# Down projection of a ConvGLU: 36 of 44 row blocks as products of seven, in one pipeline with gate and up

## The chip, the core and the metric

The kernel runs on one core of one Trainium2 chip, as one launch. The metric is the time of one execution on the device in microseconds. The profile is of one execution of the kernel before, taken by the hardware profiler. Engines are named as the profile names them: PE (TensorE; PEld are its weight loads), DVE (VectorE), ACT (ScalarE), POOL (GpSimd) and SP (SyncE). SP and POOL issue the DMAs: SP's run on the hardware queue q1, POOL's on the software queue q0.

## What is computed

One trunk layer over 512 positions of width 2048, and a last norm. The change touches the second half of it, the ConvGLU from its weights on, and the last norm:

```python
D_MODEL, SEQ = 2048, 512
D_FF = 5632                       # 44 blocks of 128

def rmsnorm(x, gain):
    return x * lax.rsqrt(jnp.mean(x * x, axis=-1, keepdims=True) + EPS) * gain

def conv_ffn(h, w_gate, w_up, conv_w, conv_b, w_down):
    a = h @ w_gate
    a_pad = jnp.pad(a, ((0, 0), (CONV_WIDTH - 1, 0), (0, 0)))
    a = sum(conv_w[j] * a_pad[:, j:j + L] for j in range(CONV_WIDTH)) + conv_b
    return (jax.nn.silu(a) * (h @ w_up)) @ w_down

# reference(): p = rmsnorm(x) @ w_in; o = concat(hgrn2(p), fox(p))
x = x + o @ w_out
h = rmsnorm(x, norm2_gain)
x = x + conv_ffn(h, w_gate, w_up, conv_w, conv_b, w_down)
return rmsnorm(x, final_norm_gain)
```

## The kernel before

All is float32. A product keeps float32's precision by splitting both operands into a high and a low part of the engine's own format (`split`: hi by ACT, lo = x - hi by DVE) and adding three matmuls: weight hi by input hi, weight hi by input lo, weight lo by input hi (`mms`, L201 to L203). Everything lies transposed, 128 features by 512 positions.

The program runs in this order. The input projection and the two mixers come first. Then `w_out`: sixteen blocks d of 128 outputs, each 16 x 3 matmuls of 512 columns; `x1_out` adds x, writes the sum to DRAM (`x1d`), squares it for the norm, and after every second d makes the "forms" of a pair of blocks.

**Gate and up** are computed as products of seven: the 2 x 2 problem of (up, gate) rows against (first, second) half of the positions, in each pair of input blocks, takes seven products in place of eight, each on a sum of weights (`s1` to `s4`, `a11`, `a12`, `a22`) and a sum of inputs (the forms `b11`, `n2`, `b21`, `t3`, `n1`, `n4`, `b22`; half the positions, 256 columns). The forms, hi and lo, stay in SBUF for the whole stage. For each of the 44 blocks f, `glu(f)` runs seven products of 8 pairs x 3 matmuls of 256 columns (L819 to L821). The four weight matrices of a block are loaded by SP, 512 KB each; `s1` and `s3` are summed by an accumulating DMA that POOL issues (L765), `s2` and `s4` by DVE (L783). `prepare(g + LEAD)` makes the weights' hi (ACT, L807) and lo (DVE, L808) two products ahead. Each f ends with the convolution, SiLU and the product with up, on DVE and ACT; both halves are multiplied by 1/rms of norm 2 there (`R2` for gate, L851, `nR2` for up, L856), split, and written to DRAM (`actd`).

**Down** reads them back. 44 blocks f in NG = 4 groups of GF = 11: for each group and each of 16 blocks d, `unit` runs 11 x 3 matmuls of 512 columns (L201 to L203, `mxt<-ot`); the weights stream in on SP as `raw<-wdn` (512 KB), and DVE adds the sum to `x1[d]`. POOL loads the activations (L886, 256 KB each) and x1 (L893). In the last group twelve d's run so; the last four d are computed with positions on the partitions (L983 to L985), one quarter of the positions at a time, while `norm` (L955 and on) normalizes and writes the quarter before.

On each engine instructions run in the order that the framework's scheduler has given them, in one queue per engine; a wait at the head of a queue holds all that stands behind it. A tile with one buffer can be loaded again only after its last reader.

Of the kernel before, what the change touches and what calls it, by code (L numbers as in the profile page):

```python
# [8 lines left out]
F32 = mybir.dt.float32  # L9
# [6 lines left out]
P = 128  # L16
# [6 lines left out]
GF = 11  # L23
NG = NF // GF
# [12 lines left out]
NPIECE_D = NF * KT * P // PIECE  # L37
QH = T // 2
KP = KT // 2
FORM = KP * P  # L40
LEAD = 2
DMA_SUMS = True
# [11 lines left out]
def tile_hymba_block(ctx: ExitStack, tc: tile.TileContext, xT, wst, wgu, wdn, wfb, consts, out, out_t):  # L54
# [71 lines left out]
    class Stream:  # L126
# [7 lines left out]
        def make(self):  # L134
# [8 lines left out]
            if self.pool is None:  # L143
                hi = self.wp.tile([P, PIECE], F32R, name="whi", tag="whi")
                lo = self.wp.tile([P, PIECE], F32R, name="wlo", tag="wlo")
            else:
                hi, lo = self.pool(F32R), self.pool(F32R)
# [518 lines left out]
    x1d = dr.tile([KT, P, T], F32, name="x1d")  # L666
    actd = dr.tile([NF, 2, P, T], F32, name="actd")
# [14 lines left out]

    tt = opened("tt", 1, "right")
    xr = opened("xr", 1, "right")
    NAMES = ("b11", "n2", "b21", "t3", "n1", "n4", "b22")
    forms = {n: [] for n in NAMES}
    acc2 = tt.tile([P, T], F32, name="acc2")

    def form(name, j, src):
        pool = tt if j < KP - 1 else tl  # L690
        hi = pool.tile([P, QH], F32R, name=f"{name}h{j}")
        lo = pool.tile([P, QH], F32R, name=f"{name}l{j}")
        s.activation(hi, src, AF.Copy)
        v.tensor_tensor(lo, src, f32(hi), op=ALU.subtract)
        forms[name].append((hi, lo))

    def pair_forms(j, ha, hb):
        b11, b12, b21, b22 = ha[:, 0:QH], ha[:, QH:T], hb[:, 0:QH], hb[:, QH:T]
# [4 lines left out]
        form("b11", j, b11)  # L703
# [3 lines left out]
        form("n1", j, n1)  # L707
        form("n2", j, n2)
        form("b21", j, b21)
        v.tensor_tensor(n2, n2, b21, op=ALU.add)  # L710
        form("n4", j, n2)
        t3 = temp()
        v.tensor_tensor(t3, b22, b12, op=ALU.subtract)
        form("t3", j, t3)
        form("b22", j, b22)
# [3 lines left out]
    def x1_out(d, ps):  # L719
# [3 lines left out]
        nc.sync.dma_start(out=x1d[d], in_=t)  # L723
# [10 lines left out]
    for d in range(WOPEN, KT):  # L734
        ps = MM()
        unit(ps, range(KT), os_)
        x1_out(d, ps)
    closed("wp", "wr", "pa")
    tl = opened("tl", 1)
    pair_forms(KP - 1, hg[-2], hg[-1])  # L740
    closed("xr")
    R2 = cp.tile([P, T], F32, name="R2", tag="R")
    nR2 = tl.tile([P, T], F32, name="nR2")

    def put2(u, r0, bc):
        s.activation(R2, bc, AF.Copy)
        s.activation(nR2, bc, AF.Copy, scale=-1.0)
# [3 lines left out]

    wf = opened("wf", 8)
    wh = opened("wh", LEAD + 2)
    gt = opened("gt", 1)
    ORDER = ("a11", "s2", "a12", "s3", "s1", "a22", "s4")
    raw = {}

    def W():
        return wf.tile([P, FORM], F32, name="wq", tag="wq")

    def load(f, name, q, q2=None):
        t = raw[f, name] = W()
        nc.sync.dma_start(out=t, in_=wgu[f, q])
        if q2 is not None:
            gp.dma_start(out=t, in_=wgu[f, q2], accum_op=ALU.add)  # L765

    def loads(f):

        if DMA_SUMS:
            load(f, "s1", 0, 1)  # L770
            load(f, "a11", 2)
            load(f, "s3", 0, 2)
            load(f, "a12", 3)
            load(f, "a22", 1)
        else:
            load(f, "a21", 0)
            load(f, "a22", 1)
            load(f, "a11", 2)
            load(f, "a12", 3)

    def add(f, name, x, y, into=None):
        t = raw[f, name] = W() if into is None else into
        v.tensor_tensor(t, raw[f, x], raw[f, y], op=ALU.add)  # L783

    def sums(f):
        if not DMA_SUMS:
            add(f, "s1", "a21", "a22")
            add(f, "s3", "a21", "a11", raw[f, "a21"])
        add(f, "s2", "s1", "a11")

    ready = {}

    def prepare(g):
        f, i = divmod(g, 7)
        if f >= NF:
            return
        if i == 0:
            sums(f)
            if f + 1 < NF:
                loads(f + 1)  # L800
        name = ORDER[i]
        if name == "s2":
            add(f, "s4", "s2", "a12")
        t = raw.pop((f, name))
        hi = wh.tile([P, FORM], F32R, name="fhi", tag="fhi")
        lo = wh.tile([P, FORM], F32R, name="flo", tag="flo")
        s.activation(hi, t, AF.Copy)  # L807
        v.tensor_tensor(lo, t, f32(hi), op=ALU.subtract)  # L808
        ready[g] = (hi, lo)

    def product(g, ps, first=True):
        prepare(g + LEAD)
        hi, lo = ready.pop(g)
        rhs = forms[NAMES[g % 7]]
        for j in range(KP):
            a, b = hi[:, j * P:(j + 1) * P], lo[:, j * P:(j + 1) * P]
            th, tl = rhs[j]
            kw = {"skip_group_check": not first}
            pe.matmul(ps, lhsT=a, rhs=th, start=(first and j == 0), stop=False, **kw)  # L819
            pe.matmul(ps, lhsT=a, rhs=tl, start=False, stop=False, **kw)  # L820
            pe.matmul(ps, lhsT=b, rhs=th, start=False, stop=(j == KP - 1), **kw)  # L821
            step()
# [4 lines left out]
    def G(name, shape=(P, T), dt=F32):  # L827
        return gt.tile(list(shape), dt, name=name, tag=name)

    def glu(f):  # L830
        cw = con[:, C_CW + 3 * f:C_CW + 3 * f + 3]
        g = 7 * f
        L, H = slice(0, QH), slice(QH, T)
        x, y, z, w = half(mm), half(mx), half(mm), half(mx)
        p1, u2, u3 = (G(n, (P, QH)) for n in ("p1", "u2", "u3"))
        a, uu = G("a"), G("uu")
        product(g, x)
        s.activation(p1, x, AF.Copy)
        product(g + 1, y)
        v.tensor_tensor(u2, p1, y, op=ALU.add)  # L840
        product(g + 2, x, first=False)
        s.activation(a[:, L], x, AF.Copy)
        product(g + 3, y, first=False)
        v.tensor_tensor(u3, p1, y, op=ALU.add)
        product(g + 4, z)
        v.tensor_tensor(uu[:, H], u3, z, op=ALU.add)
        product(g + 5, w)
        v.tensor_tensor(uu[:, L], u3, w, op=ALU.subtract)
        product(g + 6, z, first=False)
# [15 lines left out]
    loads(0)  # L865
    for g in range(LEAD):
        prepare(g)
    for f in range(NF):
        glu(f)
    closed("gt", "wh", "wf", "tl", "tt")  # L870


    wr = opened("wr", 3)
    wp = opened("wp", 4)
    pq = opened("pq", 81, "right")
    ws = Stream(wdn, NPIECE_D, wr, wp)

# [3 lines left out]
    A = X = O  # L881

    def acts_of(f):
        parts = (O(F32R), O(F32R))
        for i, part in enumerate(parts):
            gp.dma_start(out=f32(part), in_=actd[f, i])  # L886
        return parts

    acts = [acts_of(f) for f in range(GF)]
    x1 = []  # L890
    for d in range(KT):
        t = X()
        gp.dma_start(out=t, in_=x1d[d])  # L893
        x1.append(t)
    for g in range(NG - 1):
        nxt = []
        for d in range(KT):
            ps = MX()
            unit(ps, range(GF), acts)
            v.tensor_tensor(x1[d], x1[d], ps, op=ALU.add)  # L900
            if d < GF:
                nxt.append(acts_of((g + 1) * GF + d))
        acts = nxt


    x1t, g3 = [], O()

# [155 lines left out]
```

## Time and profile before

| | us |
|---|---|
| median of 3 runs | 2301.7 (2300.91 to 2302.92) |
| the profiled execution | 2302.55 |
| its span, first to last instruction | 2300.8 |
| last matmul of w_out starts / first product of gate and up starts | 897.5 / 904.7 |
| last matmul of gate and up / first of down | 1785.0 / 1787.9 |
| last matmul of down starts | 2290.5 |

The span is 1.75 us shorter than the time of the same execution; the sum of a prediction is made against 2302.55. A row of a timeline gives the start, the duration, the engine, the line and operation, the tile written and the tiles read, and in brackets the idle time before it and what ended it. Matmuls overlap, so their cost is the distance between two starts, not the duration. [...]

### The profile page before, as it was taken

The page shows a single profiled execution, that of the slowest core. Times are in us where ns is not written, and L with a number is a line of the kernel's source. Part 1 is how long each engine was busy: PE and PEld are TensorE (multiplying, and loading weights), DVE is VectorE, ACT ScalarE, POOL GpSimd, SP SyncE. Part 2 cuts the span into 40 slices and gives each one's busy share as a digit, 9 for nine tenths or more (in the row PEclk, how much of TensorE's full clock was granted, in tenths as well). Part 3 has the DMA queues.
Part 4 walks back from the last instruction along what each step waited for, and adds up shares of the span by engine and source line. Part 5 has one row for each costly group of instructions (what it writes and reads, how often), then busy time and mean ns, then how long its engine had stood idle before and what let it go on. Part 6 is the DMA issues. An engine that isn't in the chain of part 4 may idle for free.

```text
span 2300.8 us, 34411 instructions
## 1 busy us (share of the span) xinstructions
PE 2273.4 (99%) x13662; PEld 2012.7 (87%) x13662; DVE 1464.9 (64%) x2194; ACT 939.2 (41%) x1484; POOL 171.6 (7%) x259
## 2 busy tenths in 40 slices
PE   8999999999999998999999999999999999999998
PEld 7888888788888887999999999999999788888886
DVE  6666467556457565888888888888887333333345
ACT  5333233334335454544444554454444222222234
POOL 4000000000000000000000000000000512000000
PEclk9999999999999999999999999999999999999999
DMA  5222322222222455877877887878784955223223
GB/s 177 83 83 83 100 74 96 74 83 80 86 83 74 142 163 177 226 212 207 216 215 214 212 212 209 216 200 222 208 217 136 375 198 196 92 97 99 85 100 110
DMA packets 112210, 352.67 MB, mean 153 GB/s; under 512 B 12816, under 2 KB 19088, under 8 KB 112048
## 3 DMA queue, kind: packets, MB, share of 16 engines
q1 hardware_dynamic: 89568, 272.67, 36.0%
q0 software_dynamic: 22336, 77.67, 15.4%
q8 instruction: 107, 1.75, 0.3%
q14 instruction: 55, 0.45, 0.1%
q10 hardware_dynamic: 144, 0.12, 0.0%
HBM read 318.96 MB, written 31.46 MB: 152 GB/s over the span
## 4 chain that ended last, share of the span: by engine, by line
PE 95%; DMA 2%; DVE 1%; issue 1%; ACT 0%; POOL 0%; DVEq 0%; ACTq 0%; POOLq 0%
PE pq L819 12%; PE pq L820 12%; PE pq L821 12%; PE mmt L201 9%; PE mmt L203 9%; PE mmt L202 9%; PE mxt L202 7%; PE mxt L201 7%; PE mxt L203 7%; PE mmt L286 2%; PE mmt L284 2%; PE mmt L285 2%; DMA ot<-actd 1%; DMA wq<-wgu 1%; DMA raw<-wdn 1%
## 5 line engine op out<-in xcount | busy, mean ns | idle before, releaser
L150 DVE TENSOR_TENSOR wlo<-raw,whi 128x512 fp32r<-128x512 f32 x453 | 316.3, 699 | 464.5 <-ACT whi L149 424.9
L149 ACT ACTIVATE whi<-raw 128x512 fp32r<-128x512 f32 x453 | 284.8, 630 | 686.3 <-PE mxt L202 322.2
L807 ACT ACTIVATE fhi<-wq 128x1024 fp32r<-128x1024 f32 x308 | 326.6, 1061 | 365.7 <-PE pq L820 323.0
L808 DVE TENSOR_TENSOR flo<-wq,fhi 128x1024 fp32r<-128x1024 f32 x308 | 376.3, 1222 | 58.2 <-ACT fhi L807 52.4
L201 PE MATMUL mmt<-at,whi 128*128 128x512 f32 x896 | 354.8, 396 | 0.0
L203 PE MATMUL mmt<-at,wlo 128*128 128x512 f32 x896 | 349.8, 390 | 0.0
L202 PE MATMUL mmt<-at,whi 128*128 128x512 f32 x896 | 349.3, 390 | 0.0
L201 PE MATMUL mxt<-ot,whi 128*128 128x512 f32 x660 | 262.2, 399 | 2.9 <-ACT whi L149 2.7
L202 PE MATMUL mxt<-ot,whi 128*128 128x512 f32 x660 | 261.8, 397 | 0.5 <-DMA ot<-actd 0.5
L203 PE MATMUL mxt<-ot,wlo 128*128 128x512 f32 x660 | 261.6, 397 | 0.5 <-DVE wlo L150 0.5
L203 PEld LDWEIGHTS mmt<-at,wlo 128*128 128x128 f32 x896 | 168.2, 188 | 35.9
L201 PEld LDWEIGHTS mmt<-at,whi 128*128 128x128 f32 x896 | 168.3, 188 | 34.9 <-issue 1.9
L202 PEld LDWEIGHTS mmt<-at,whi 128*128 128x128 f32 x896 | 168.4, 188 | 33.1
L201 PEld LDWEIGHTS mxt<-ot,whi 128*128 128x128 f32 x660 | 124.5, 189 | 34.8 <-ACT whi L149 2.9
L202 PEld LDWEIGHTS mxt<-ot,whi 128*128 128x128 f32 x660 | 124.6, 189 | 31.8 <-DMA ot<-actd 2.1
L203 PEld LDWEIGHTS mxt<-ot,wlo 128*128 128x128 f32 x660 | 124.7, 189 | 30.6 <-DVE wlo L150 1.0
L765 POOL DMA_DIRECT2D wq<-wgu x88 | 75.9, 862 | 782.1 <-DVE flo L808 388.1
L783 DVE TENSOR_TENSOR wq<-wq 128x1024 f32<-128x1024 f32 x88 | 107.5, 1222 | 3.5 <-DMA wq<-wgu 2.0
L286 PE MATMUL mmt<-wlo,at 128*128 128x512 f32 x256 | 100.6, 394 | 4.4 <-DVE wlo L150 4.4
L819 PE MATMUL pq<-b11h,fhi 128*128 128x256 f32 x352 | 100.2, 285 | 3.6 <-ACT fhi L807 3.6
L284 PE MATMUL mmt<-whi,at 128*128 128x512 f32 x256 | 101.7, 397 | 0.3 <-ACT whi L149 0.3
L821 PE MATMUL pq<-b11h,flo 128*128 128x256 f32 x352 | 99.9, 284 | 1.3 <-DVE flo L808 1.3
(303 smaller groups left out, 5067.7 us busy)
## 6 DMA issues: line engine op xcount, KB each, us to landing
wq<-wgu SPq DMA_DIRECT2D x220, 512.0 KB, 4.5
raw<-wst SPq DMA_DIRECT2D x143, 512.0 KB, 3.5
wq<-wgu POOLq DMA_DIRECT2D x88, 512.0 KB, 7.3
raw<-wdn SPq DMA_DIRECT2D x87, 512.0 KB, 3.5
ot<-actd POOLq DMA_DIRECT2D x88, 256.0 KB, 6.6
actd<-ah SPq DMA_DIRECT2D x44, 256.0 KB, 3.2
actd<-al SPq DMA_DIRECT2D x44, 256.0 KB, 3.0
xt<-xT SPq DMA_DIRECT2D x16, 256.0 KB, 5.3
```

What stands on the lines that cost most here:

```text
L149: s.activation(hi, src, AF.Copy)
L150: v.tensor_tensor(lo, src, f32(hi), op=ALU.subtract)
L201: pe.matmul(ps, lhsT=a, rhs=xh[:, ts], start=(first and i == 0), stop=False)
L202: pe.matmul(ps, lhsT=a, rhs=xl[:, ts], start=False, stop=False)
L203: pe.matmul(ps, lhsT=b, rhs=xh[:, ts], start=False, stop=(last and i == n - 1))
L284: pe.matmul(pss[i], lhsT=xh[:, ts], rhs=hi, start=(k == 0), stop=False)
L286: pe.matmul(pss[i], lhsT=xh[:, ts], rhs=lo, start=False, stop=(k == KT - 1))
L807: s.activation(hi, t, AF.Copy)
L808: v.tensor_tensor(lo, t, f32(hi), op=ALU.subtract)
L819: pe.matmul(ps, lhsT=a, rhs=th, start=(first and j == 0), stop=False, **kw)
L820: pe.matmul(ps, lhsT=a, rhs=tl, start=False, stop=False, **kw)
L821: pe.matmul(ps, lhsT=b, rhs=th, start=False, stop=(j == KP - 1), **kw)
```

## The change

Gate, up and most of down form one pipeline of "units" (`class Seven`): 44 units of gate and up of 7 x 8 x 3 matmuls, then 24 units of down of 7 x 6 x 3 matmuls, all of 256 columns. Down's first 36 row blocks are 18 pairs, in three chunks of six pairs; a unit is one pair of output blocks (m, in the order 6, 7, 0 to 5) of one chunk. Its weight sums are all made on DVE. Its inputs are seven forms of the activations: `forms_out` makes them after each second f and writes them to DRAM (`formd`), and they come back through POOL's queue (`load_form`) into the buffers in which gate and up's forms stood. There is one buffer for each form, so a form of the next chunk is loaded once the product of the chunk's last unit that reads it is through: seven forms, hi and lo, 786 KB each, 11.0 MB per chunk. What a unit gives is added to `yd` in DRAM by an accumulating DMA; in chunk 0 `xi` (x1, multiplied by the rms of norm 2, with its sign turned in the even blocks) is written to `yd` first. The multiplication of up by 1/rms is gone; the last norm applies it. The other 8 row blocks run as before (8 x 3 matmuls of 512 columns for each of twelve d, then the late four). Loads of gate and up's weights are issued in two halves, into 2 + 5 buffers in place of 8.

```diff
-GF = 11
-NG = NF // GF
+FL = 8
+NPIECE_D = FL * KT * P // PIECE
+CHUNKS = (6, 6, 6)
+DORDER = (6, 7, 0, 1, 2, 3, 4, 5)
...
+    class Seven:
+        def loads(self, u, early):
+            src, n, dma_sums = self.units[u]
+            if dma_sums:
+                todo = (("a11", 2), ("s1", 0, 1)) if early else (("a12", 3), ("s3", 0, 2), ("a22", 1))
+            else:
+                todo = (("a11", 2), ("a21", 0)) if early else (("a12", 3), ("a22", 1))
+            for name, q, *more in todo:
+                t = self.tile(u, name)
+                nc.sync.dma_start(out=t, in_=src[q])
+                for q2 in more:
+                    gp.dma_start(out=t, in_=src[q2], accum_op=ALU.add)
...
+        def prepare(self, g):
+            u, i = divmod(g, 7)
+            if i == 0 and not dma_sums:
+                self.sum(u, "s1", "a21", "a22")
+                self.sum(u, "s3", "a21", "a11", into="a21")
+            s.activation(hi, t, AF.Copy)
+            v.tensor_tensor(lo, t, f32(hi), op=ALU.subtract)
+            if i == 0:
+                self.sum(u, "s2", "s1", "a11", into="a11")
+                self.loads(u + 1, True)
+            elif i == 1:
+                self.sum(u, "s4", "s2", "a12", into="s2")
+            elif i == (4 if dma_sums else 3):
+                self.loads(u + 1, False)
...
+    def parts_out(src, n, dst):
+        for i in range(2):
+            t = G("oh" if i == 0 else "ol", (P, 4, QH), F32R)[:, 0:n]
+            if i == 0:
+                hi = t
+                s.activation(t, src, AF.Copy)
+            else:
+                v.tensor_tensor(t, src, f32(hi), op=ALU.subtract)
+            nc.sync.dma_start(out=dst(i), in_=f32(t))
+    def forms_out(p, r):
+        v.tensor_tensor(r[:, 4], r[:, 0], r[:, 1], op=ALU.subtract)
+        v.tensor_tensor(r[:, 1], r[:, 3], r[:, 1], op=ALU.subtract)
+        yield KP
+        v.scalar_tensor_tensor(r[:, 5], r[:, 4], -1.0, r[:, 3], op0=ALU.mult, op1=ALU.subtract)
+        v.tensor_tensor(r[:, 6], r[:, 5], r[:, 2], op=ALU.add)
+        for a, b in ((0, 4), (4, 7)):
+            parts_out(r[:, a:b], b - a, lambda i: formd[c][a:b, i, :, j].rearrange("s p t -> p s t"))
+            yield 2 * KP
+    def load_form(c, name):
+        t = slot(name)
+        for i, part in enumerate(t):
+            gp.dma_start(out=f32(part[:, 0:n]), in_=formd[c][SLOTS.index(name), i])
...
-        v.tensor_tensor(uu, uu, nR2, op=ALU.mult)
-        hi, lo = G("ah", dt=F32R), G("al", dt=F32R)
-        s.activation(hi, uu, AF.Copy)
-        v.tensor_tensor(lo, uu, f32(hi), op=ALU.subtract)
-        for i, part in enumerate((hi, lo)):
-            nc.sync.dma_start(out=actd[f, i], in_=f32(part))
+        if f >= 2 * NPAIR:
+            parts_out(r[:, b:b + 2], 2, lambda i: actd[f - 2 * NPAIR, i])
+        elif f % 2:
+            start(forms_out(f // 2, r))
...
+    def down(c, m, forms, nxt):
+        if c == 0:
+            xi = G("xi", (P, 2, T))
+            gp.dma_start(out=xi, in_=x1d[m])
+            v.scalar_tensor_tensor(xi[:, 0], xi[:, 0], -1.0, rms, op0=ALU.mult, op1=ALU.mult)
+            v.tensor_tensor(xi[:, 1], xi[:, 1], rms, op=ALU.mult)
+            nc.sync.dma_start(out=yd[m], in_=xi)
+        sv.product(x, forms)
+        next_form(nxt, c + 1, 0)
...
+        gp.dma_start(out=yd[m], in_=o, accum_op=ALU.add)
...
-    acts = [acts_of(f) for f in range(GF)]
-    for d in range(KT):
-        gp.dma_start(out=t, in_=x1d[d])
-    for g in range(NG - 1):
-        for d in range(KT):
-            unit(ps, range(GF), acts)
-            v.tensor_tensor(x1[d], x1[d], ps, op=ALU.add)
+    for f in range(FL):
+        for i, part in enumerate(acts[-1]):
+            gp.dma_start(out=f32(part), in_=actd[f, i])
+    for d in (12, 0, 4, 8):
+        for b in range(2):
+            gp.dma_start(out=y4[:, 2 * b:2 * b + 2], in_=yd[d // 2 + b])
...
-    start(norm(i, ps, ys, 6 if i < 3 else 0))
+    start(norm(i, ps, FL + 3 if i < 3 else 0))
```

SP's queue, from the end of w_out to the first weights of gate and up, before. `wq` are weight tiles, `x1d` is the sum after w_out:

```order
L142 DMA raw<-wst 128x1024 [waits DMAHW4_49,DVE_49]
L723 DMA x1d<-xr 128x512 [waits DMAHW0_49,DVE_49]
L763 DMA wq<-wgu 128x1024 [waits PE_49]
L723 DMA x1d<-xr 128x512 [waits DVE_49]
L763 DMA wq<-wgu 128x1024 [waits DMAHW3_49]
```

And after, where `wc` is the tile of `a11`:

```order
L143 DMA raw<-wst 128x1024 [waits DMAHW4_49,DVE_49]
L740 DMA x1d_5869<-xr 128x512 [waits DMAHW0_49,DVE_49]
L790 DMA wc<-wgu 128x1024 [waits PE_49]
L790 DMA wq<-wgu 128x1024
L790 DMA wq<-wgu 128x1024 [waits DMAHW3_49]
L790 DMA wq<-wgu 128x1024
```

The first load of all is now that of `a11`, the second that of `s1`; the wait of the first is for the last matmul of w_out, where before it was for one some 2 us earlier. The last write of x1 stands behind seven loads.

POOL's queue at the end of gate and up, before: all 88 accumulating loads, then the activations of the first group, x1, and the rest.

```order
L765 DMA wq<-wgu 128x1024 x88
L886 DMA ot<-actd 128x512 x22
L893 DMA ot<-x1d 128x512 x16
L886 DMA ot<-actd 128x512 x66
```

And after, from the same place into the second unit of chunk 0 (`formd_5879` is chunk 0's, h and l are hi and lo):

```order
L792 DMA wq<-wgu 128x1024 x88
L905 DMA b11l<-formd_5879 128x1536
L905 DMA b11h<-formd_5879 128x1536
L905 DMA n2h<-formd_5879 128x1536
...
L905 DMA b22h<-formd_5879 128x1536
L905 DMA b22l<-formd_5879 128x1536
L975 DMA xi<-x1d_5868 128x1024
L1003 DMA yd_5876<-o 128x1024
L975 DMA xi<-x1d_5869 128x1024
L975 DMA xi<-x1d_5862 128x1024
```

The fourteen loads of forms (those of `b21`, `t3`, `n1` and `n4` are left out) are followed by the first `xi`; the second `xi` stands behind the accumulation of the first unit's result. At the two later chunk seams the fourteen loads stand behind the accumulation of the last unit but one:

```order
L1003 DMA yd_5874<-o 128x1024
L905 DMA b11l<-formd_5880 128x1536
L905 DMA b11h<-formd_5880 128x1536
...
L905 DMA b22l<-formd_5880 128x1536
L1003 DMA yd_5875<-o 128x1024
```

DVE's queue in chunk 0, in the fourth unit (`flo` are lo parts of weights, L800 sums of weights, `u` and `o` sums of products):

```order
L818 TENSOR_TENSOR flo<-wc,fhi 128x768 [waits Activation_49]
L800 TENSOR_TENSOR wc<-wq,wc 128x768 [waits DVE_49]
L996 TENSOR_TENSOR o<-u_18561,pq 128x256 [waits DMASW1_49,PE_49]
L976 SCALAR_TENSOR_TENSOR xi<-xi,rms 128x512 [waits DMAHW4_49,DMASW5_49]
L818 TENSOR_TENSOR flo<-wc,fhi 128x768 [waits Activation_49]
L999 TENSOR_TENSOR o<-u_18561,pq 128x256 [waits PE_49]
L800 TENSOR_TENSOR wc<-wc,wq 128x768 [waits DMAHW2_49,DVE_49]
L977 TENSOR_TENSOR xi<-xi,rms 128x512
```

The multiplication of `xi` waits for a DMA of POOL, and the sums and lo parts that the next products need stand behind it.

## Rows read from the trace of the kernel before

**Rows 1.** The page: span, busy time and share by engine, the chain by engine.

```profile
span 2300.8 us, 34411 instructions
PE 2273.4 (99%) x13662; PEld 2012.7 (87%) x13662; DVE 1464.9 (64%) x2194; ACT 939.2 (41%) x1484; POOL 171.6 (7%) x259
...
PE 95%; DMA 2%; DVE 1%; issue 1%; ACT 0%; POOL 0%; DVEq 0%; ACTq 0%; POOLq 0%
```

**Rows 2.** Timeline of PE in down: two starts, twenty matmuls of 512 columns apart.

```profile
2000.20 0.40 PE L203 MATMUL mxt<-ot,wlo 128*128 128x512 f32 x1
...
2004.87 0.40 PE L202 MATMUL mxt<-ot,whi 128*128 128x512 f32 x1
```

**Rows 3.** Timeline of PE in gate and up: a hundred matmuls of 256 columns apart.

```profile
1200.06 0.28 PE L819 MATMUL pq<-n1h,fhi 128*128 128x256 f32 x1
...
1211.90 0.28 PE L820 MATMUL pq<-n2l,fhi 128*128 128x256 f32 x1
```

**Rows 4.** Table by stretch: length, busy time of each engine, PEclk, DMA share, GB/s.

```profile
1000.00:1700.00 700.00, 700.00 (x5918) 700.00 (x5917) 586.96 (x704) 349.92 (x422) 60.36 (x70) 1.00 0.80 213
1790.00:1795.00 5.00, 5.00 (x13) 3.63 (x13) 2.64 (x5) 1.33 (x3) 3.52 (x7) 0.50 0.98 329
1785.00:1860.00 75.00, 71.15 (x287) 54.47 (x286) 27.12 (x41) 18.69 (x30) 42.77 (x80) 0.95 1.02 383
1850.00:2000.00 150.00, 150.00 (x645) 120.67 (x644) 49.69 (x73) 34.03 (x54) 14.92 (x28) 1.00 0.45 155
2266.00:2290.00 24.00, 24.00 (x109) 19.70 (x108) 13.82 (x33) 14.39 (x46) 0.00 (x0) 1.00 0.37 108
```

**Rows 5.** The chain at the seam from w_out to gate and up (start, us, what).

```profile
895.63 3.28 DMA wq<-wgu
...
899.49 9.21 DMA wq<-wgu
...
908.73 1.23 DVE wq L783
...
912.44 0.39 PE pq L821
```

**Rows 6.** Timeline of DVE there: the sum with w_out's last block.

```profile
897.91 0.69 DVE L722 TENSOR_TENSOR xr<-xr,mmt 128x512 f32<-128x512 f32 x1 [8.45 <-PE mmt L203]
```

**Rows 7.** DVE by line and form, 1000 to 1700: busy us, mean ns.

```profile
L808 DVE TENSOR_TENSOR flo<-wq,fhi 128x1024 fp32r<-128x1024 f32 x247 | 301.9, 1222 | 45.4 <-ACT fhi L807 40.7
...
L855 DVE SCALAR_TENSOR_TENSOR t<-a,con,t 128x510 f32<-128x510 f32 x35 | 26.2, 750 | 1.2
...
L856 DVE TENSOR_TENSOR uu<-uu,nR 128x512 f32<-128x512 f32 x35 | 24.2, 692 | 1.2
...
L846 DVE TENSOR_TENSOR uu<-u,pq 128x256 f32<-128x256 f32 x35 | 14.7, 421 | 22.4 <-PE pq L821 22.4
```

**Rows 8.** DMA queues and issues, 1785 to 1860: MB, share of 16 engines; KB, us to landing.

```profile
q0 software_dynamic: 6386, 20.94, 75.0%
q1 hardware_dynamic: 2269, 7.72, 26.5%
...
ot<-actd POOLq DMA_DIRECT2D x64, 256.0 KB, 6.6
```

**Rows 9.** The same, 1000 to 1700.

```profile
q0 software_dynamic: 10080, 36.70, 30.2%
...
wq<-wgu POOLq DMA_DIRECT2D x70, 512.0 KB, 7.3
```

**Rows 10.** Timeline of PE at the seam to down: idle time ahead, then the granted clock.

```profile
1787.94 0.50 PE L201 MATMUL mxt<-ot,whi 128*128 128x512 f32 x1 [2.67 <-ACT whi L149]
...
1794.88 0.58 PE L202 MATMUL mxt<-ot,whi 128*128 128x512 f32 x1
1795.29 0.39 PE L203 MATMUL mxt<-ot,wlo 128*128 128x512 f32 x1
```

**Rows 11.** Timeline of PE at the end: the last matmul of down.

```profile
2290.53 0.39 PE L985 MATMUL mxt<-ot 128*128 128x512 f32 x1
```

More of the change, by code (lines that the diff above doesn't have):

```diff
@@ L665, in tile_hymba_block @@
     dr = opened("dr", 1, space=bass.MemoryType.DRAM)
-    x1d = dr.tile([KT, P, T], F32, name="x1d")
-    actd = dr.tile([NF, 2, P, T], F32, name="actd")
+    x1d = [dr.tile([P, 2, T], F32, name=f"x1d{m}") for m in range(KP)]
+    yd = [dr.tile([P, 2, T], F32, name=f"yd{m}") for m in range(KP)]
+    actd = dr.tile([FL, 2, P, T], F32, name="actd")
+    formd = [dr.tile([7, 2, P, n, QH], F32, name=f"formd{c}") for c, n in enumerate(CHUNKS)]
     os_ = {}
@@ L741, in tile_hymba_block @@
+    sv = Seven()
+    for f in range(NF):
+        sv.add([wgu[f, q] for q in range(4)], KP, True)
+    for c, n in enumerate(CHUNKS):
+        for m in DORDER:
+            sv.add([wd7[c, m, q] for q in range(4)], n, False)
+    sv.prepare(0)
+    x1_out(KT - 1, ps)
+    pair_forms(KP - 1, hg[-2], hg[-1], lambda: sv.prepare(1))
     closed("xr")
     R2 = cp.tile([P, T], F32, name="R2", tag="R")
-    nR2 = tl.tile([P, T], F32, name="nR2")
+    rt2 = cp.tile([P, 4], F32, name="rt2")
     def put2(u, r0, bc):
@@ L746, in put2 @@
         s.activation(R2, bc, AF.Copy)
-        s.activation(nR2, bc, AF.Copy, scale=-1.0)
+        v.tensor_tensor(rt2, u, r0, op=ALU.mult)
     start(rms_stats([acc2], put2, 5))
-    wf = opened("wf", 8)
-    wh = opened("wh", LEAD + 2)
     gt = opened("gt", 1)
[L755 to L789, printed above, removed]
@@ L811, in product @@
[L811 to L822, printed above, removed]
@@ L865, in tile_hymba_block @@
-    loads(0)
-    for g in range(LEAD):
-        prepare(g)
-    for f in range(NF):
[L869 to L875, printed above, removed]
-    ws = Stream(wdn, NPIECE_D, wr, wp)
+        if f >= 2 * NPAIR:
+            parts_out(r[:, b:b + 2], 2, lambda i: actd[f - 2 * NPAIR, i])
+        elif f % 2:
+            start(forms_out(f // 2, r))
+    dforms = {}
+    for f in range(NF):
+        glu(f, dforms if f == NF - 1 else None)
@@ L878, in O @@
+    for c in range(len(CHUNKS)):
+        nxt = {}
+        for i, m in enumerate(DORDER):
+            end = i + 1 == len(DORDER)
+            if end and c + 1 == len(CHUNKS):
+                while ws.made < 3:
+                    ws.make()
+            down(c, m, dforms, nxt if end and c + 1 < len(CHUNKS) else None)
+        dforms = nxt
+    closed("tt")
+    pq = opened("pq", 33, "right")
+    yp = opened("yp", 1, "right")
     def O(dt=F32, shape=(P, T)):
         return pq.tile(list(shape), dt, name="ot", tag="q")
-    A = X = O
@@ L1014, in _weights @@
     head, parts = parts, []
-    for g in range(NG):
-        rows = w_down[g * GF * P:(g + 1) * GF * P]
-        nd = KT if g + 1 < NG else ND
-        parts += [cols(rows, d * P, P) for d in range(nd)]
-        parts += [cols(rows, nd * P, D - nd * P)] if nd < KT else []
+    rows = w_down[2 * NPAIR * P:]
+    parts += [cols(rows, d * P, P) for d in range(ND)]
+    parts += [cols(rows, ND * P, NLATE * P)]
     def rows_of(parts):
```

301 lines of the change are left out of this document (198 added, 103 removed).

## The prediction

> **What bounds the kernel now.** I read the page first, for who is busy: PE 2273.4 of 2300.8 us, 99%, and 95% of the chain [rows 1]. DVE has 64%, ACT 41%. So a change pays by the matmul time that it takes off PE, less what makes PE wait. Next the pitch of matmuls, start to start: twenty of 512 columns in down take 2004.87 - 2000.20 = 4.67 us, 0.2335 each [rows 2]; a hundred of 256 columns in gate and up 11.84 us, 0.1184 each [rows 3]. Then the table by stretch, for the margin that other engines have beside such matmuls: in gate and up DVE is busy 587 of 700 us (84%) and the DMA engines 80%, with PE never idle; in down DVE has 33% and DMA 45% [rows 4]. Down thus has room for more DVE work; the question is whether the forms arrive in time. For that I read the queues at the seam into down, where much is loaded at once: 383 GB/s, with every DMA engine busy [rows 4], 20.94 MB on the software queue and 7.72 MB on the hardware queue in 75 us [rows 8].
>
> **The change part by part**, against the profiled execution's 2302.55 us.
>
> *Matmuls.* Removed: 36 x 16 x 3 = 1728 of 512 columns, 1728 x 0.2335 = 403.5 us. Added: 24 units x 7 x 6 x 3 = 3024 of 256 columns, 3024 x 0.1184 = 358.0. Together **-45.5**, all of it on the path. The new ones have the form of those of gate and up (the same three, a weight tile of 128 x 128 each), so I take their pitch; half of 0.2335 would give 5 us more.
>
> *Seam from w_out to gate and up.* The first load of s1 is issued at 895.63 and the accumulation onto it takes 9.21 us; s2 and a lo part follow, and PE runs on from 912.44 [rows 5]. Now a11 goes first and waits for w_out's last matmul, through when its sum begins at 897.91 [rows 6]; s1 follows at about 898.2, 2.6 us later than before. Some of it comes back, since fewer loads compete with the accumulation (7.3 us is the median elsewhere [rows 9]). Range 0 to +4, taken **+2**.
>
> *Gate and up.* Per f the product with nR2 (0.69) falls away. Per pair, four sums of 256 (some 0.42 each), a lo part of 1024 (1.22) and one of 768 (0.96, between the 692 ns of 512 and the 1222 of 1024) replace two lo parts of 512 [rows 7]: 1.68 + 2.18 - 1.38 - 1.38 = 1.1 us per pair, 0.55 per f. DVE had 16.7 of 19.9 us, and gets 17.3. Writes grow from 0.52 to 0.92 MB per f, in pieces of 1 KB, beside a DMA share of 0.80. PE waited for nothing with the old load, so **+1**; to +10 if the accumulated sums come late.
>
> *Forms.* Each chunk loads 11.0 MB through POOL's queue. A form's buffer is free when the last unit's product with it is through: the first 18 matmuls (24 at the end of gate and up) into that unit. Counted in PE's new order, the last form of the next chunk is first read 247 matmuls later, 29.2 us, at a chunk seam, and 260, 30.8 us, at the first. From below: at the whole 383 GB/s the seven forms need 28.7 us, a wait of 0 to 1. From above: at what the software queue moved beside the hardware queue, 20.94 MB / 75 us = 279 GB/s, they need 39.4 us, a wait of 10.2; at a chunk seam the accumulation of the last unit but one stands ahead of them (0.52 MB at 36.70 MB / (0.302 x 700 us) = 174 GB/s per full share [rows 9], 3 us), so 13; at the first seam the wait from this end is 8.6, with 2 MB of other loads and writes beside it (5 us) 14. The hardware queue's demand is near the same as in that row: a unit's weights are 1.57 MB in 14.9 us, 105 GB/s, against 103 there. But PE's own wait stops that demand, and the hardware queue's 4 KB pieces went at 7.72 MB / (0.265 x 75 us) = 388 GB/s per full share against 372 for the software queue's 2 KB ones [rows 8]; forms come in 6 KB pieces. So I take 9 at each chunk seam and 10 at the first, nearer to the upper end. [...] Sum **+28**, between 1 and 41.
>
> [...]
>
> *DVE in down.* A unit has eleven operations of 768 (seven lo parts, four sums) at 0.96 and five of 256 from PSUM at 0.42: 12.6 of 14.9 us. In chunk 0 xi adds 0.75 + 0.69: 14.1 of 14.9, 94%. There every xi waits in DVE's queue for a load by POOL, which waits for the write of the xi before it (one buffer) and in the second unit stands behind an accumulation (7.3 us [rows 9]). Behind it stand lo parts that PE needs within two products, 4.3 us. No row shows such a wait. Bounds 0 and +10; with 0.8 us to spare per unit I take **+4** for chunk 0 and **+1** for the other two.
>
> *Seam into the last eight row blocks.* The old seam into down lost 9 to 10 us: 2.67 idle, half clock to 1795.29, then waits for activations at 6.6 us to landing [rows 8, 10]. The new one has 16 loads of activations in place of 22, of which all but the first stand behind the last accumulation; PE mixes three d's to fill the waits. -4 to +4, taken **-1**.
>
> *End.* After the last matmul some 10.3 us remain (2290.53 to 2300.8 [rows 1, 11]). A late quarter now has 24 matmuls in place of 33, 5.4 us; DVE was busy 13.8 of 24 us there [rows 4], 4.3 us per quarter of 7.5, and gets a little more per norm, so it runs close to PE and the last norm may start late: 0 to +5, taken **+2**.
>
> Sum: -45.5 + 2 + 1 + 28 + 4 + 1 - 1 + 2 = -8.5, 2294.0 against 2302.55. The median of the runs lies 0.85 below the profiled execution, so **2293** is forecast, 0.4% faster. Matmuls alone would bring 2%; the seams take most of it back.
>
> **The rivals.**
>
> *Forms hidden.* The software queue gets nearly the full 383 GB/s, since weights are loaded a unit ahead and may wait. Then the seams cost 1 us each, 3 in place of 28: -33.5, 2269, or 2268 as a median. For it: every DMA engine was busy in that row, so the forms take whatever weights leave. Against: a unit's sums of weights are made two products ahead and need all four matrices; weights can't wait 10 us.
>
> *Forms queue behind weights, slower than before.* One mechanism: at each seam the software queue has 279 GB/s or less for as long as the forms last, and PE waits at n1 and b22. Price 14 + 13 + 13 = 40, and 2 us at half clock for each; xi in chunk 0 comes behind the late forms and DVE can't catch up at 94%: +8 in place of +4. The tail at +3: -45.5 + 2 + 1 + 46 + 8 + 1 - 1 + 3 = +14.5, 2317, as a median 2316. It decides from 37 us of seams on, 12 each, all else as forecast. For it: the 75.0% and 26.5% of one row [rows 8] are this very mix. [...] Against it: that row lasts 75 us of constant demand, a seam some 35, in part of which PE stands still and asks for no weights.
>
> *The pitch isn't that of gate and up.* If DMA or DVE traffic slowed every matmul by 3% (0.122), +11 us: no change or a little slower, 2304. Against it: gate and up have the same traffic and more.
>
> **How the numbers follow.** Forecast 0.50, with its own range 2286 to 2302; forms hidden 0.20; forms behind weights 0.26; the pitch 0.04. The bound of no change is 0.2%, 4.6 us, about what a measurement of this kernel tells from none: faster means below 2297.1, slower above 2306.3. Of the forecast two thirds lie below 2297, the rest within; with the first rival, faster gets 0.33 + 0.20 = 0.53. The second rival gives 0.20 above and 0.06 within; slower 0.22 with a part of the pitch, same 0.25. The range 2267 to 2318 leaves out nearly half of the first rival and of the second each, 2 in 10.
>
> **What would show it.** Right: a pitch of 0.118 in the units of down; PE idle for 8 to 12 us at each of the three seams, ended by DMAs into n1, n4 or b22; DVE at 90% or more in chunk 0 with waits for xi of 1 to 2 us; none in chunks 1 and 2 past their seams. The seams are told by the software queue's GB/s: 300 or more is the forecast, above 360 the first rival, 279 and below the second. Wrong at the root would be waits in gate and up, where formd's small writes meet the accumulating loads, since 44 units of 0.3 us there are 13 us; or PE at half clock over whole units of chunk 0.

## The result and the profile after

The changed kernel takes 2466.05 us (median of 4 runs, 2463.08 to 2469.72) against 2301.51: 1.0715 times as long, with a 95% interval of 1.0696 to 1.0733. The forecast was 2293, 0.4% faster, in a range that ended at 2318. It missed by 173 us.

The page's totals, which answer to [rows 1]: span, busy time by engine, the chain by engine and by line (the profile follows it back only over the last fifth of the program here, from 1978 us on).

```profile
span 2465.6 us, 37368 instructions
PE 2308.1 (94%) x14958; PEld 2117.2 (86%) x14958; DVE 1637.4 (66%) x2437; ACT 999.1 (41%) x1523; POOL 177.8 (7%) x253
...
PE 8%; DMA 5%; DVE 4%; issue 2%; ACT 1%; DVEq 0%; POOL 0%; ACTq 0%; POOLq 0%
DMA wq<-wd 4%; DVE flo L818 2%; PE pq L841 1%; PE pq L842 1%; PE pq L843 1%; PE mxt L203 1%; PE mxt L204 1%; PE mxt L202 1%; DMA t3l<-formd 1%; DVE wc L800 1%; DVE wq L800 1%; ACT fhi L817 1%; DMA yd<-xi 0%; PE mxt L1128 0%; PE mxt L1129 0%
```

PE stands still for 157 us, where it was 27, and its mean granted clock (PEclk, a share of full speed) fell from 0.994 to 0.966. First I ask where, by the starts of the first product of each block on PE's timeline; gate and up end with the end of their last product:

| stretch | before | changed | difference | forecast |
|---|---|---|---|---|
| span's start to the end of block f = 0 | 930.3 | 935.5 | +5.3 | +2 |
| the other 43 blocks of gate and up | 854.8 | 961.4 | **+106.6** | +1 |
| down and the end | 515.7 | 568.6 | **+52.9** | -11.5 |

The table by stretch says how gate and up lose it (columns as in [rows 4]): the first row is a stretch in which forms are written, the second one in the last eight blocks, which make no forms.

```profile
1000.00:1400.00 400.00, 370.16 (x2949) 368.57 (x2948) 300.45 (x372) 177.72 (x212) 30.22 (x35) 0.95 0.77 203
1800.00:1850.00 50.00, 50.00 (x421) 50.00 (x420) 39.01 (x47) 25.11 (x32) 4.32 (x5) 1.00 0.81 212
```

No engine is busier than before (DVE 75% from 1000 to 1400, where [rows 4] have 84%, ACT 44% and 50%), the DMA engines neither (0.77 and 0.80); with forms, PE waits and its clock is 0.95, and without them it neither waits nor slows. Of the 106.6 us, 62 are PE's waits and 8 the slower pitch of which more below; the other 36 are left for matmuls at a lower clock after the waits (in the run below that has none of them the clock is 1.00). PE's timeline at the first matmul of three blocks in a row:

```profile
1090.96 0.28 PE L841 MATMUL pq<-b11h,fhi 128*128 128x256 f32 x1
...
1117.71 0.37 PE L841 MATMUL pq<-b11h,fhi 128*128 128x256 f32 x1
...
1137.86 0.28 PE L841 MATMUL pq<-b11h,fhi 128*128 128x256 f32 x1
```

One block takes 26.7 us, the next 20.1. It is so for all 18 pairs: every second block takes 24.4 to 27.2. The waits of ACT over gate and up, and those of PE, name the place (engine, line waited for, us in total, times, longest):

```profile
ACT oh L884 <- DMA formd<-oh: 87.0, 18, 6.2
```

```profile
PE pq L841 <- DVE r L938: 62.1, 18, 4.7
```

And one of the eighteen, on the timelines of ACT, DVE and PE:

```profile
1097.74 1.04 ACT L884 ACTIVATE oh<-r 128x1024 fp32r<-128x1024 f32 x1
...
1106.60 0.85 ACT L884 ACTIVATE oh<-r 128x768 fp32r<-128x768 f32 x1 [5.62 <-DMA formd<-oh]
1107.35 1.04 ACT L817 ACTIVATE fhi<-wc 128x1024 fp32r<-128x1024 f32 x1
```

```profile
1108.43 1.23 DVE L818 TENSOR_TENSOR flo<-wc,fhi 128x1024 fp32r<-128x1024 f32 x1 [5.38 <-ACT fhi L817]
```

```profile
1112.45 0.55 PE L841 MATMUL pq<-b22h,fhi 128*128 128x256 f32 x1 [4.13 <-DVE r L938]
```

ACT copies the first four forms into `oh` at 1097.74. The next three need the same buffer, so at the head of ACT's queue their copy waits 5.62 us, until the write of the first four to DRAM has landed. Behind it stands the hi part of a weight (`fhi`); DVE stands behind that with its lo part, and behind this on DVE a sum that frees the accumulator PE wants.

Down loses its time in another queue. Its row in the table by stretch, the waits of DVE from 1930 to 2320, and one of them:

```profile
1897.00:2350.00 453.00, 392.35 (x3024) 384.66 (x3023) 293.97 (x403) 153.63 (x219) 40.64 (x62) 0.94 0.63 192
```

```profile
DVE wq L800 <- DMA wq<-wd: 69.8, 19, 5.7
```

```profile
2124.68 0.96 DVE L800 TENSOR_TENSOR wq<-wq 128x768 f32<-128x768 f32 x1 [4.66 <-DMA wq<-wd]
```

SP's timeline ahead of it, and the transfer that DVE waited for, from the chain:

```profile
2116.37 10.49 SPq L790 DMA_DIRECT2D wq<-wd  x3
```

```profile
2117.57 6.99 DMA wq<-wd
```

That sum is `s1` of the next unit, of a21 and a22. SP's three loads take 10.5 us to issue, since each waits for one of the five common buffers. By the program's order the second of them is a22's: it goes out at 2117.57, when DVE has read its buffer for a lo part of the unit before, and lands 7.0 us later. DVE was through with all that stands ahead of the sum at 2120.02, 4.66 us before it could begin. Away from the seams a unit takes 16.0 to 22.5 us in place of 14.9. The longest, in chunk 0, also has a wait of DVE for `xi`, 5.1 us.

The three seams, on which the prediction had spent most of its words, cost some 17, 8 and 7 us (two units at each, less 15.1 us apiece, the time of a unit that waits for nothing); 10, 9 and 9 were forecast.

### The profile page after: what moved, and what is told of

Read it like the earlier page. It is cut to its first block, busy times and chain, and to the rows that moved or that the text cites. A ratio compares the mean times of both kernels' runs of the same rounds, so it can differ in the third digit from the quotient of the medians.

```text
span 2465.6 us, 37368 instructions
## 1 busy us (share of the span) xinstructions
PE 2308.1 (94%) x14958; PEld 2117.2 (86%) x14958; DVE 1637.4 (66%) x2437; ACT 999.1 (41%) x1523; POOL 177.8 (7%) x253
## 5 line engine op out<-in xcount | busy, mean ns | idle before, releaser
L817 ACT ACTIVATE fhi<-wq 128x1024 fp32r<-128x1024 f32 (+1 forms) x272 | 267.1, 983 | 323.9 <-PE pq L842 245.7
L817 ACT ACTIVATE fhi<-wc 128x1024 fp32r<-128x1024 f32 (+1 forms) x204 | 200.5, 983 | 413.6 <-DVE wc L800 234.1
L818 DVE TENSOR_TENSOR flo<-wc,fhi 128x1024 fp32r<-128x1024 f32 (+1 forms) x204 | 230.3, 1129 | 174.9 <-ACT fhi L817 172.5
L818 DVE TENSOR_TENSOR flo<-wq,fhi 128x1024 fp32r<-128x1024 f32 (+1 forms) x272 | 306.1, 1127 | 37.7 <-ACT fhi L817 37.3
L841 PE MATMUL pq<-b22h,fhi 128*128 128x256 f32 x496 | 162.4, 327 | 103.9 <-DVE r L938 62.1
L842 PE MATMUL pq<-b22l,fhi 128*128 128x256 f32 x496 | 159.8, 322 | 0.0
L843 PE MATMUL pq<-b22h,flo 128*128 128x256 f32 x496 | 159.4, 321 | 0.0
L842 PE MATMUL pq<-t3l,fhi 128*128 128x256 f32 x496 | 141.7, 286 | 4.6 <-DMA t3l<-formd 4.6
L841 PE MATMUL pq<-n2h,fhi 128*128 128x256 f32 x496 | 140.0, 282 | 5.3 <-ACT fhi L817 5.3
L842 PE MATMUL pq<-b11l,fhi 128*128 128x256 f32 x496 | 143.5, 289 | 0.0
```

The lines of the kernel that those rows point to most:

```text
L842: pe.matmul(ps, lhsT=a, rhs=tl_, start=False, stop=False, **kw)
L843: pe.matmul(ps, lhsT=b, rhs=th, start=False, stop=(j == n - 1), **kw)
```

## The experiments

Theory A: gate and up lose their time to the one buffer `oh`, with ACT's queue behind it. Theory C: down's units lose theirs to a22's buffer. Rivals: the new split of the weight loads (B); the write itself, slow by its pieces of 1 KB (A1) or by the weight loads ahead of it in SP's queue (A3); DVE's load (D). A time given without an interval is that of one execution; four of the changed kernel spread over 6.6 us.

**The forms of three pairs only.**

```diff
-            nc.sync.dma_start(out=dst(i), in_=f32(t))
+            for o in dst(i):
+                nc.sync.dma_start(out=o, in_=f32(t))
...
-        elif f % 2:
+        elif f % 2 and f // 2 % CHUNKS[0] == 0:
             start(forms_out(f // 2, r))
```

> The changed kernel, but the forms of the activations are made for 3 of 18 pairs only (the first of each chunk) and written six times, so the down projection reads the same pair six times over; nothing else differs, gate and up's loads in two halves and 2 + 5 buffers stay. Theory A: the 113 us that gate and up lose come from making and writing forms (every second f takes 25 us in place of 20). Then 15 pairs run at 20 us, and the kernel takes 2466 - 15 x 5.2 = about 2388 (2375 to 2400; the three pairs that write six times may lose more). Rival B: they come from the new split of the weight loads, or from fewer buffers. Then every second f stays at 25 us: 2455 to 2470.

Measured 2427.89. The fifteen pairs without forms take 20.1 us for every block, the three that write six times lose 20 to 21 us each. A stretch between them:

```profile
1100.00:1200.00 100.00, 100.00 (x839) 100.00 (x839) 76.98 (x91) 46.22 (x56) 8.63 (x10) 1.00 0.72 184
```

The time is above the range since the three pairs lost 61 us in all, where 16 were allowed; the blocks decide, for A against B.

**The write in rows of 4 KB.**

```diff
-    formd = [dr.tile([7, 2, P, n, QH], F32, name=f"formd{c}") for c, n in enumerate(CHUNKS)]
+    formd = [dr.tile([n, 2, P, 7, QH], F32, name=f"formd{c}") for c, n in enumerate(CHUNKS)]
...
```

> The changed kernel with formd laid out so that a write of four forms is 4 KB in a row for each partition, in place of four pieces of 1 KB (the loads of forms then read pieces of 1 KB). Theory A1: ScalarE's second copy waits because the write of the one buffer takes 6.8 us, and it takes that long because of its 1 KB pieces. Then a write lands in 4 us or less, ScalarE waits 2 us in place of 5 for each pair, every second f takes 21 to 22 us: 2400 to 2420, less some us more at the three seams where forms are loaded. Theory A2: it takes that long because the transfer shares the DMA engines with weights; then it lands in 6 to 7 us as before and the time is 2455 to 2480.

Measured 2469.55; a write of four forms lands after 6.6 us (6.8 before), ACT waits 84.9 us in all (87.0). The small pieces are not the cause.

**Pieces of two through two buffers.**

```diff
-            t = G("oh" if i == 0 else "ol", (P, 4, QH), F32R)[:, 0:n]
+            t = G("oh" if i == 0 else "ol", (P, 2, QH), F32R, bufs=2)[:, 0:n]
...
-        for a, b in ((0, 4), (4, 7)):
+        for a, b in ((0, 2), (2, 4), (4, 6), (6, 7)):
...
```

> The changed kernel with the seven forms split and written as pieces of two (2, 2, 2, 1) through two buffers of two, in place of pieces of four and three through one buffer of four: the same memory. Theory A: one buffer is what ScalarE waits for, with weights' hi parts standing behind it. Then a piece finds a free buffer and 256 KB land in 4 to 5 us; waits go from 5 us to 0 to 2 for each pair, every second f takes 20 to 22 us: 2375 to 2420. If the third and fourth pieces wait for the first two as long as the second piece waits now: 2450 to 2480.

Measured 2452.94: 13 us less, and short of what theory A promised. Writes of half the size take 6.2 us to land, so the third and fourth pieces wait for the first two: 72.0 us in 29 waits.

**The hi parts' write from ACT's own queue.**

```diff
-            nc.sync.dma_start(out=dst(i), in_=f32(t))
+            (s if i == 0 else nc.sync).dma_start(out=dst(i), in_=f32(t))
```

> The changed kernel with the writes of the forms' hi parts issued by ScalarE, on a DMA queue of its own, in place of SyncE, whose queue also carries the weight loads. Theory A3: a write of 256 KB took 6.2 us where one of 512 KB took 6.8, and rows of 4 KB took 6.6, so it isn't its own bytes that take the time but the weight loads ahead of it in the same queue. Then it lands in 3 to 4 us, ScalarE's waits go from 87 us to under 40, and every second f from 25.3 to 22 us: 2400 to 2425. If the DMA engines share out evenly anyway, it lands in 6 to 7 us and nothing changes: 2455 to 2480.

Measured 2505.31, 39 us more: the write takes 8.8 us there, and ACT waits 110.2 us for it in 17 waits up to 1760 (87.0 in 18 in the changed kernel). So the weights ahead of it in SP's queue are not what it waits for either; a queue of its own made it later. Why 512 KB take 6.6 to 8.8 us to write beside the weights is left open; that they do so whatever the rows and the queue is enough here.

**Two buffers of four.** The hi parts and the lo parts on their way to DRAM get two buffers each; DVE's lo copies had waited for theirs only once, 1.9 us. The memory comes from the weights' parts (3 buffers in place of 4).

```diff
-    wh = opened("wh", LEAD + 2)
+    wh = opened("wh", LEAD + 1)
...
-            t = G("oh" if i == 0 else "ol", (P, 4, QH), F32R)[:, 0:n]
+            t = G("oh" if i == 0 else "ol", (P, 4, QH), F32R, bufs=2)[:, 0:n]
...
```

> The changed kernel with two buffers of four forms each for the hi and lo parts on their way to DRAM, in place of one; the memory comes from the weights' parts, which get 3 buffers in place of 4. Theory A: ScalarE no longer waits for a write, and every second f takes 20 to 21.5 us: 18 x 4 to 5 us less, 2375 to 2395. If VectorE's wait for the tile of sums (r7, one buffer) is the limit by itself, f keeps 23 us and more: 2420 to 2460. The third buffer of parts costs 0 to 0.3 us a unit if products are made early enough.

Measured 2368.46, 98 us less. Every block takes 20.1 us; ACT's wait for `oh` is gone, with the same writes taking 6.7 us. A is shown: not the write's length, but that the one buffer held up ACT's queue for it.

```profile
1000.00:1400.00 400.00, 400.00 (x3350) 399.97 (x3349) 337.46 (x419) 199.70 (x240) 34.49 (x40) 1.00 0.84 231
```

**Own buffers for a22 in down.**

```diff
+            if name == "a22" and u > NF:
+                pool, tag, bufs = wx, "wx", 2
...
-    wr = opened("wr", 2)
-    wp = opened("wp", 3)
+    wx = opened("wx", 2)
+    wr = opened("wr", 1)
+    wp = opened("wp", 2)
...
```

> The changed kernel with two buffers more for down's weights: a22 has a tag of its own there, in place of one of the five common buffers (to make room, one buffer of the late row blocks' raw weights and one pair of their parts fewer). Theory C: a unit of down takes 18 us in place of 15 because a22's load waits for a buffer of the unit before, and lands 4 to 7 us after VectorE wants it for the first sum. Then VectorE's waits for weights (70 us in all) go to under 15, a unit takes 15.0 to 15.5 and the kernel 2400 to 2425. Rival D: VectorE with 84% has no room, or the transfers themselves are late; then units stay at 17 to 18 us and the time at 2450 to 2475.

Measured 2448.97, 17 us less, between the two ranges. Units without a seam take 15.1 us, as C says, but for two in chunk 0 (15.9 and 20.2), and the last matmul of the chunks starts at 2308.8 in place of 2350.2: 41 us. But the last eight row blocks then take 23 us more, since I had taken the memory from their weights. DVE's waits from 1930 to 2330 no longer name a22 or `wq`; this is what is left of weights in them:

```profile
DVE wq L803 <- DMA wc<-wd: 1.3, 2, 0.7
```

**The same without that loss.** As above, but with the memory from the weights' parts and the last row blocks' buffers kept.

> The changed kernel with two own buffers for a22 in down as in the run before, but with all buffers of the late row blocks kept; the memory comes from the weights' parts (3 in place of 4). Theory C: units of down take 15.1 us as they did there, and the last eight row blocks the 106 us of the changed kernel, not 130: 2466 - 41 = 2420 to 2430, gate and up unchanged. If the shorter units only moved the loss to the end, 2440 to 2455.

Measured 2441.51: the last eight row blocks are as in the changed kernel and units take 15.1, but gate and up takes some 12 us more. PE's waits there now end at the weights' hi and lo parts themselves (47.2 and 25.7 us from 900 to 1780, 7.6 and 0.8 in the changed kernel from 900 to 1760), as if with three buffers of parts PE were closer behind ACT when `oh` blocks it; no run shows that by itself. The expectation had called gate and up unchanged; that was wrong.

**Both, and the tile of sums split.** Both edits, and `r7` as a tile of four and one of three.

> The changed kernel with both cures (two buffers of four forms, two own buffers for a22 in down, 3 buffers of weights' parts) and the tile of seven sums split in a tile of four and one of three, so that the next pair's sums needn't wait for the last three to be read. Theory A and C together: gate and up 20.1 us per f (97 us less), units of down 15.1 (60 us less with what the seams keep, 17 + 8 + 7 us): 2300 to 2330, about the time of the kernel before; the seams where forms are loaded are then what is left of the loss. If a cause is missing, 2340 and up.

Measured 2328.17, 1.0111 times the kernel before (1.0094 to 1.0128): 138 of the 164 us are the two cures. (The split tile adds nothing that shows: blocks took 20.1 us without it, and 138 is the 98 of two buffers and some 40 of a22's.) PE's timeline at the second seam shows what stays, each row with the idle time ahead of it:

```profile
1946.24 0.36 PE L844 MATMUL pq<-n2h,fhi 128*128 128x256 f32 x1 [0.49 <-DMA n2h<-formd]
1948.99 0.58 PE L845 MATMUL pq<-n2l,fhi 128*128 128x256 f32 x1 [2.39 <-DMA n2l<-formd]
...
1957.65 0.39 PE L845 MATMUL pq<-t3l,fhi 128*128 128x256 f32 x1 [1.44 <-DMA t3l<-formd]
...
1963.04 0.58 PE L845 MATMUL pq<-n1l,fhi 128*128 128x256 f32 x1 [2.41 <-DMA n1l<-formd]
```

```profile
1940.00:1975.00 35.00, 25.17 (x166) 23.03 (x165) 16.40 (x22) 8.41 (x12) 3.53 (x6) 0.90 0.91 353
```

A form's lo part lands after its hi part and PE waits for each, product after product; the waits are short, but the clock is 0.90 over the stretch. With quick units the seams cost 17, 15 and 15 us, 47 in all, where they cost 31 with slow ones.

**Forms loaded for the first chunk only.**

```diff
-            forms[NAMES[i]] = load_form(c, NAMES[i])
+            forms[NAMES[i]] = load_form(c, NAMES[i]) if c == 0 else dforms[NAMES[i]]
```

> The kernel with both cures and the split tile (2328 us), with the loads of forms at the second and third chunk left out: all three chunks read the first chunk's forms, so the down projection takes a third of the activations three times. Theory F: what those two seams still cost, 15.0 and 14.7 us beyond their units' 15.1, is the forms' 11.0 MB at some 415 GB/s with the weights beside them. Then the seams go to 0 to 2 us and the kernel to 2298 to 2304. Rival G: it is the turn from one chunk to the next by itself, the scheduled order and VectorE's queue; then 2320 to 2330.

Measured 2302.89, 25 us below the kernel that it is made from. From the sixth unit of chunk 0 to the end every unit takes 15.1 us, across both turns of chunk:

```profile
1900.00:2180.00 280.00, 280.00 (x2336) 280.00 (x2334) 221.40 (x299) 120.41 (x168) 17.36 (x21) 1.00 0.56 139
```

So the two later seams are the forms' transfer (F), and not the turn of chunk. The first seam, 17 us in both kernels, is not settled by this: of its 12.5 us of waits in the kernel with both cures only 2.4 end at a form's load, the others at parts and sums of ACT and DVE, and why these come late there is open.

**What is left: the pitch.** Where nothing waits, a block of gate and up takes 20.07 us after the change and 19.88 before; 44 blocks are 8 us that no wait explains. Two guesses: where the matmuls' inputs stand, and where their weights stand. (The changed kernel opens one small tile more ahead of the weights, `rt2`.)

```diff
-        hi = pool.tile([P, QH], F32R, name=f"{name}h{j}")
-        lo = pool.tile([P, QH], F32R, name=f"{name}l{j}")
...
+            hi, lo = (x[:, j] for x in slots[name])
...
```

> The kernel before with one edit: the seven inputs of a form stand in one tile each for hi and lo, as in the changed kernel, in place of a tile of 1 KB for each. In the changed kernel a block f of gate and up takes 20.07 us where nothing is waited for, before 19.88; 44 of them are 8 us. Theory E: the pitch of the matmuls depends on where their inputs stand. Then a block takes 20.0 to 20.1 here too, and the kernel 2308 to 2312. Rival: it comes from something else that the change moved (weights' buffers, the program around it); then 19.88 and 2300 to 2304.

Measured 2303.33, 1.0002 times before (0.9993 to 1.0012), and 19.88 a block: not the tiles of the inputs.

```diff
+    pad = opened("pad", 1).tile([P, 8], F32, name="pad")
+    gp.memset(pad, 0.0)
     wf = opened("wf", 8)
...
```

> The kernel before with 32 bytes of memory taken ahead of the weight buffers of gate and up, so that all of them begin 32 bytes further on; nothing else. In the kernel before the weights' parts begin at an address that leaves 32 when divided by 64, in the changed kernel one that leaves 0, and a block f takes 19.88 us there and 20.07 here. Theory H: the weights' place sets the pitch. Then a block takes 20.0 to 20.1 and the kernel 2308 to 2312. Rival: the place doesn't matter; 19.88 and 2300 to 2304.

Measured 2311.10, 1.0038 times before (1.0023 to 1.0052), and 20.09 a block: 32 bytes of memory make the kernel before 8 us slower. Of the tiles that they move PE reads only the weights' parts; the raw weights and the tiles of the sums, which ACT, DVE and the DMAs use, move with them. The opposite test, the same 32 bytes on the kernel with both cures:

> The kernel with both cures and the split tile (2328 us) with the same 32 bytes ahead of its weight buffers, so that they leave 32 as in the kernel before. Theory H: a block of gate and up goes from 20.07 to 19.88 us, a unit of down from 15.1 to 14.95: 8.4 + 3.6 us less, 2314 to 2318. Rival: 2326 to 2331.

Measured 2317.08, 11 us below 2328.17 and 1.0063 times before (1.0048 to 1.0078); blocks take 19.93 and units 14.8. Its matmuls recorded in the stretch that had 5863 of them without the 32 bytes, in the same 700 us:

```profile
1000.00:1700.00 700.00, 700.00 (x5904) 700.00 (x5903) 593.68 (x737) 353.37 (x425) 60.35 (x70) 1.00 0.85 232
```

No kernel of these beats the one before.

## Why the prediction was wrong

*What bounds the kernel.* Right as far as it went: PE bounds it. The room on DVE and on the DMA engines was read from busy shares, and neither engine became busier: DVE has 84% in gate and up in [rows 4] and 75% there in the changed kernel, the DMA engines 0.80 and 0.77. The loss came from the order of queues and from buffers, which no share shows.

*Gate and up, +1 with +10 as the upper end: +107.* This step of the prediction failed, and most of the miss is here. The working counted the added operations (0.55 us of DVE per f) and the added bytes, and then took over "PE waited for nothing" from a kernel without these writes. It didn't count the copies that the step itself issues on ACT, nor that the second needs the first one's buffer back. The rows had nearly what was needed: 6.6 and 7.3 us from issue to landing for loads of 256 and 512 KB on a loaded queue [rows 8, 9]; the two copies stand one product, 3 us, apart in ACT's order. As an estimate, the difference of 3.6 to 4.3 us, at the head of a queue that also makes the weights' parts, 18 times, gives +65 to +77. Measured were 62 us of PE's waits; the 36 us at a lower clock would still have been missing, since the sum has no term for the clock here. That the prediction named waits in gate and up as what would be wrong at the root, by small pieces of 1 KB meeting the accumulating loads, hit the place and missed the cause: with pieces of 4 KB ACT still waited 84.9 us, where it was 87.0.

*VectorE in down, +4 and +1: some +59.* The second step that failed. The chunks took 453 us, 95 more than 24 x 14.92; the seams have 31 of it and the pitch 4. Its 12.6 us of work per unit were near: with a22's own buffers DVE is busy 11.8 us of a unit (46.89 of 60 us from 2100 to 2160), and the work fits units of 15.1 us. What the step lacked was the count of buffers: a unit takes four tiles of five, so the last load of the next can't be issued before DVE has made lo parts of this one. The first rival even said that weights are loaded a unit ahead and may wait; a22's load is not. The wait that the step did price, DVE's for `xi`, came out as priced: in the kernel with both cures two units of chunk 0 take 19.0 and 16.2 us, together 4.9 more than at 15.1, beside these waits of DVE from 1770 to 2330:

```profile
DVE xi L981 <- DMA xi<-x1d: 10.6, 5, 3.4
```

*Matmuls, -45.5.* The count was right, the pitch 1% off: 15.1 us for 126 is 0.1198, +4.4 us, and gate and up paid 8 us of the same kind, for which the sum had no term. Both went, all but 0.05 us a block, with the 32 bytes on the kernel with both cures: 19.93 us a block and 14.8 a unit.

*Seams, +28.* In the changed kernel some 31; the likely reason isn't in the working: slow units gave the loads time. Once units ran at their pace, the seams took 47. That is near the second rival's 46, and that kernel's 2328 is near the rival's 2316 and the 12 or 13 us of the pitch, but the rival's number was met by luck: it asks for a software queue at 279 GB/s or less and waits of 13 to 14 us. The forecast's own signs came out instead. PE is idle for 12.5, 9.8 and 9.2 us at the three seams, where 8 to 12 were given, though at the later two the waits end at n2, t3 and n1, not at n4 or b22. At the second seam the software queue moved 9.77 MB from 1940 to 1972, when the last form had landed: 305 GB/s, where 300 or more was the forecast. What was too low was the price of the clock: the forecast's sum has no term for it, where the second rival has 2 us a seam. Between waits of 0.3 to 2.4 us PE ran at a granted clock of 0.90 on the mean, so its slow matmuls were on the path, some 5 us, about a third of each seam. (The range's upper end for the three, 41, should be 40 by its own terms.)

The DMA queues also moved more than the mean of 383 GB/s in [rows 4]: at the second seam they ran at 404 to 426 GB/s for 27 us, as the DMA table from 1940 to 1985 shows in 40 slices.

The slices (GB/s), and the two queues from 1940 to 1972 (packets, MB, share of the 16 engines):

```profile
GB/s 423 410 418 418 412 412 426 412 421 421 412 404 418 421 415 418 407 418 404 407 415 408 415 407 382 278 231 93 29 18 0 0 0 0 7 63 157 282 211 276
```

```profile
q0 software_dynamic: 1839, 9.77, 78.1%
q1 hardware_dynamic: 933, 2.52, 20.5%
```

*Seam from w_out, +2 with +4 as its end: +5.* The accumulation onto s1 was issued at 903.45 in place of 899.49, 4 us later, not 2.6: the load of s1, issued 2.6 us later, took 4.7 us to land in place of 3.3, with the loads of five more tiles issued right behind it.

*The last eight row blocks and the end, +1: some +3.* From 2350.3 to 2465.6, with 384 matmuls and the last norm; PE waits 6.4 us for the first activations. No experiment took this apart.

*What eats the saving once both causes are cured.* Against the profiled execution before, that kernel's span is 29.7 us longer (2330.5 and 2300.8). The terms add up to some 29: -45.5 of matmuls, +13 of pitch, +47 of seams, +5 of `xi`, +6 at the seam from w_out, +3.5 at the end.

## What to carry to other kernels

When a change adds a copy to an engine's queue, ask three things of it before its duration: which buffer it writes, who has to be done with that buffer, and what stands behind it in the queue. A buffer that leaves by DMA is busy for the landing time, here 7 us, not for the copy's 1 us, and a busy share of 41% says nothing about a queue that stands still. Count the buffers of a pipeline against the tiles of one unit; here, with one to spare, the last load of the next unit was on the path, and DVE's first sum waited up to 5.7 us for it.

## What the runs showed of the chip that was not expected

The pitch of matmuls changed by 1% with a shift of 32 bytes of the tiles in memory. Opened at one place, 168 matmuls of 256 columns took 20.07 to 20.09 us, 32 bytes off it 19.88 to 19.93; the 32 bytes alone made the kernel before 1.0038 times as long, and the same step took 11 us off the changed kernel with its cures. My estimate, counted from the tiles opened ahead as if each took a multiple of 32 bytes, is that the slower place of the weights is a multiple of 64 bytes; the traces hold no addresses, so no run shows it. In the kernel before the weights' parts are all that PE reads of what was moved, so their place is the likely cause, but it was not tried alone. Why one place is the slower is open.

The DMA engines moved 404 to 426 GB/s for 27 us, with the software and the hardware queue at work, above the mean of 383 over 75 us in the kernel before.

With waits of 0.3 to 2.4 us, one for nearly every product, the granted clock was 0.90 over the 35 us of the second seam, where it was 1.00 over the 280 us of the kernel with the forms loaded once in which PE waits for nothing; the slow matmuls cost some 5 us there, about half as much as the 9.8 us of waits.
